# The attention mix in fp32 on half-width columns of the array, with V and the scores kept whole instead of in two parts

## The chip, the cores and the metric

The kernel runs on one core of a Trainium2 chip. The time is the device time of one launch in microseconds: the median of three runs for the kernel before is 313.22 us (313.04 to 313.24).

The core has five engines with a queue each: PE (TensorE, the matmuls; PEld is its weight load), DVE (VectorE), ACT (ScalarE), POOL (GpSimd) and SP (which here issues the loads of the weights). They meet through semaphores.

## The reference

One transformer layer over 256 tokens, 1024 wide, 16 heads of 64, all in fp32. One MoBA block is 256 long, so only a token's own block remains and the attention is plain causal attention with a relative-position bias:

```
y   = rms_norm(x, attn_norm)
qkv = y @ w_qkv                                   # 1024 x 3072
s   = q @ k.T / 8 + rel_bias[bucket(i - j)]       # causal, per head
p   = softmax(s);   o = p @ v
h   = x + o @ w_o
u   = causal_conv3(rms_norm(h, ffn_norm) @ w_up) + conv_b      # 1024 x 5632
h   = h + (silu(gate) * val) @ w_down             # 2816 x 1024
out = rms_norm(h, final_norm)
```

## The kernel before

The large matmuls run in fp32r, a one-pass form of the matmul with a shortened mantissa. To keep nearly all of fp32, each operand is split into two parts: ACT writes a high part (rounded to fp32r), DVE writes the low part (value minus high part), and PE sums three products: high by high, high by low, low by high. The weights come from HBM in 1 MB pieces (`raw`, issued by SP), and each half piece is split by `split_hi` (L141, ACT, tile `whi`) and `split_lo` (L154, DVE, tile `wlo`) some steps ahead of their use. All instructions stand in the order in which the code writes them; there is no scheduler.

The stages: the V projection (256 tokens by 1024, in four PSUM accumulators), then a loop over the eight pairs of heads (p = 0 to 7), then the output projection, then the FFN and the last norm.

In step p of the loop PE runs `project(p, 0)` (Q of the pair, 24 matmuls of 256 columns), `mix(p-3)`, `scores(p-1)`, `project(p, 1)` (K, 24 matmuls) and `flip(p-2)`. After the loop, `mix(5)`, `scores(7)`, `flip(6)`, `mix(6)`, `flip(7)` and `mix(7)` stand among the matmuls of the output projection (`o_part`). So five mixes in the loop and `mix(5)` after it are followed by a `scores`; `mix(6)` is followed by a `flip`, `mix(7)` by `o_part`.

What these do:

- `scores(p)` is four true fp32 matmuls (tiles `qt`, `kt`): for each of the two heads of the pair, one with 128 and one with 256 moving columns. A head has 64 channels, so each matmul uses 64 of the array's 128 rows; head 0 takes the lower half, head 1 the upper. The trace has two PE records for each fp32 matmul (two passes, each with its own weight load), so eight for a pair. DVE adds the bias and takes the row maximum (L401, L405), ACT takes the exponential (L410), and `normalise` divides by the sum on DVE (L414, L418).
- `flip(p)` transposes the pair's scores: six fp32 transposes on PE (L423 to L425) into a two-bank PSUM tile; ACT copies them to the high part of `pt` (L427), DVE makes the low part (L428).
- `mix(p)` multiplies by V. The stationary operand is the pair's 128 columns of V (both heads), in a high and a low part (`vs`, 2 parts x 2 token blocks x 1024); the moving operand is the flipped scores of both heads side by side (512 columns for the first 128 keys, 256 for the last 128, which only later queries see). Three part products of two matmuls make six. Each head's result is then half of the output: rows 0 to 63 of head 0's columns and rows 64 to 127 of head 1's; the other halves are not used. Four evictions, ACT two (L443, high part of `ot`) and DVE two (L445, low part), each on 64 partitions.

`vs` itself is written after the V projection by four ACT (L350) and four DVE (L351) instructions. `pt` has one buffer.

Of the kernel before, what the change touches and what calls it, by code (L numbers as in the profile page):

```python
# [8 lines left out]
F32 = mybir.dt.float32  # L9
F32R = mybir.dt.float32r  # L10
BF16 = mybir.dt.bfloat16
AF = mybir.ActivationFunctionType
ALU = mybir.AluOpType

P = 128
S = 256
NT = S // P
D = 1024
KD = D // P
H = 16  # L20
HD = 64
NP = H // 2
# [16 lines left out]
def bucket_of(d):  # L39
    exact = BUCKETS // 2  # L40
    if d < exact:
        return d
    big = exact + int(math.log(d / exact) / math.log(MAX_DIST / exact) * (BUCKETS - exact))
    return min(big, BUCKETS - 1)
# [3 lines left out]
def tile_block(ctx: ExitStack, tc, x, attn_norm, w_qkv, w_o, rel_bias, ffn_norm, w_up, conv_w,  # L48
               conv_b, w_down, final_norm, out):
    nc = tc.nc  # L50
# [12 lines left out]
    def acc():  # L63
        return psA.tile([P, 512], F32, name="acc")

    def bank():
        return psW.tile([P, 512], F32, name="bank")

    def two_banks():
        return psT.tile([P, 1024], F32, name="twobank")  # L70

    def mm(o, lhsT, rhs, start, stop):
        nc.tensor.matmul(o, lhsT, rhs, start=start, stop=stop, skip_group_check=True)  # L73
# [169 lines left out]
    def rstds():  # L243

        r = small.tile([P, NT], F32, name="rstd")
        nc.vector.scalar_tensor_tensor(r, stat[:, 0, :], D * EPS, stat[:, 1, :], op0=ALU.add, op1=ALU.add)
        nc.gpsimd.tensor_tensor(r, r, minus_half.to_broadcast([P, NT]), op=ALU.pow)
        return r

    def spread(d, ps):  # L250

        for t in range(NT):
            mm(ps[:, t * P:(t + 1) * P], ones, d[t], True, True)
        return ps[:, :S]

    def diagonals(r):
        d = [small.tile([P, P], F32, name=f"diag{t}", bufs=1) for t in range(NT)]
        for t in range(NT):
            nc.vector.tensor_scalar(d[t], ident, r[:, t:t + 1], None, op0=ALU.mult)
        return d  # L260
# [31 lines left out]
    while d1 >= 0:  # L292
        b = bucket_of(d1)
# [3 lines left out]
        n = d1 - d0 + 1  # L297
# [6 lines left out]

    att = ctx.enter_context(ExitStack())
    ap = att.enter_context(tc.tile_pool(name="ap", bufs=1))
    vs = ap.tile([P, 2, NT, D], F32R, name="vs")
    ot = ap.tile([P, 2, NP, S], F32R, name="ot")
    ap.tile([P, 48], F32, name="skew")
    rk, rq = (ap.tile([P, S], F32, name=n) for n in ("rk", "rq"))  # L310
# [19 lines left out]
    accs = {c: acc() for c in CHAINS}  # L330
# [3 lines left out]
    for i in range(4):  # L334
# [8 lines left out]
        if i == 2:  # L343
            nc.scalar.activation(junk[1], xt[1], AF.Square, accum_out=stat[:, 0, 1:2])
            r1 = rstds()
            d1 = diagonals(r1)
    ps = spread(d1, bank())
    for t, half in CHAINS:
        c = slice(half * 512, (half + 1) * 512)
        nc.scalar.activation(vs[:, 0, t, c], accs[t, half], AF.Copy, scale=r1[:, t:t + 1])  # L350
        nc.vector.scalar_tensor_tensor(vs[:, 1, t, c], accs[t, half], r1[:, t:t + 1], vs[:, 0, t, c].bitcast(F32),  # L351
                                       op0=ALU.mult, op1=ALU.subtract)
    nc.vector.tensor_copy(rk, ps)
    nc.vector.tensor_scalar(rq, rk, HD ** -0.5, None, op0=ALU.mult)
    unit(2)
# [6 lines left out]
    def backwards(a):  # L362

        (step, n), _ = a.ap
        return bass.AP(tensor=a.tensor, offset=a.offset + P - 1, ap=[[step, n], [P, NT], [-1, P]])

    qt, kt, sc, pt, bias, sums = {}, {}, {}, {}, {}, {}
# [52 lines left out]
    def flip(p):  # L420
        ps = two_banks()
        for a in range(2):
            nc.tensor.transpose(ps[:, a * S:a * S + P], sc[p][:, a, 0:P], ident)  # L423
            nc.tensor.transpose(ps[:, a * S + P:(a + 1) * S], sc[p][:, a, P:2 * P], ident)  # L424
            nc.tensor.transpose(ps[:, 512 + a * P:512 + (a + 1) * P], sc[p][:, a, 2 * P:], ident)  # L425
        pt[p] = ap.tile([P, 2, 768], F32R, name="pt", bufs=1)
        nc.scalar.activation(pt[p][:, 0, :], ps[:, :768], AF.Copy)  # L427
        nc.vector.tensor_tensor(pt[p][:, 1, :], ps[:, :768], pt[p][:, 0, :].bitcast(F32), op=ALU.subtract)  # L428

    def mix(p):  # L430
        ps = acc() if p < NP - 2 else bank()
        c = slice(p * P, (p + 1) * P)
        late = ps.rearrange("p (a q) -> p a q", a=2)[:, :, P:]
        for n, (i, j) in enumerate(((0, 0), (1, 0), (0, 1))):
            mm(ps, vs[:, i, 0, c], pt[p][:, j, :512], n == 0, False)
            mm(late, vs[:, i, 1, c], pt[p][:, j, 512:].rearrange("p (a q) -> p a q", a=2), False, n == 2)
        for i in range(2):
            for a in range(2):
                r = slice(a * HD, (a + 1) * HD)
                o = backwards(ps[r, a * S:(a + 1) * S])  # L440
                h, l = (ot[r, n, p, :].rearrange("p (t q) -> p t q", t=NT) for n in range(2))
                if i == 0:
                    nc.scalar.activation(h, o, AF.Copy)  # L443
                else:
                    nc.vector.tensor_tensor(l, o, h.bitcast(F32), op=ALU.subtract)  # L445

# [4 lines left out]
    for p in range(NP):  # L453
        split_to(("qk", p))
        project(p, 0)
        if p >= 3:
            mix(p - 3)
        if p >= 1:
            scores(p - 1)
            unit_lo()  # L460
        project(p, 1)
        if p == 0:
            other_params()
        if p >= 2:
            flip(p - 2)
        if p >= 1:
            normalise(p - 1)
            unit_hi()
        unit()
        if p + 2 < NP:  # L470
            load_bias(p + 2)
        split_to(("qk", p), AHEAD)

    accs = {}
# [7 lines left out]

    o_part(0, 0, range(0, 5))
    mix(NP - 3)
    scores(NP - 1)
    unit_lo()
    flip(NP - 2)
    normalise(NP - 1)
    unit_hi()
    o_part(1, 0, range(0, 5))  # L490
    o_part(0, 0, [5])
    o_part(1, 0, [5])
    mix(NP - 2)
    split_to(("up", 0))
    flip(NP - 1)
    o_part(0, 1, range(0, 5))
    o_part(1, 1, range(0, 4))
# [38 lines left out]
    accs = {}  # L536
# [71 lines left out]
    ps = spread(diagonals(rstds()), acc())  # L608
# [3 lines left out]
    for j in range(NF):  # L612
# [7 lines left out]
        i = (j - 3) // 2  # L620
# [87 lines left out]
```

## Time and profile before

| | |
|---|---|
| median of three runs | 313.22 us (313.04 to 313.24) |
| the profiled execution | 312.95 us, of which the span is 311.2 us |
| PE busy | 302.1 us (97%) |
| DVE busy, ACT busy | 241.8 us (78%), 179.7 us (58%) |
| granted clock of PE over the span | 0.996 |

The span is the time from the first to the last instruction of the profiled execution. A matmul's record is longer than what it adds to a row of matmuls, since they are pipelined: what one costs in a row is the distance from its start to the start of the next. The timeline merges neighbouring records that share names; its second column runs from the first record's start to the last one's end.

### The profile page before, as it was taken

Reading aid. Unit: us, or ns where it says so; the run is one execution under the profiler, and the core shown is the slowest. Engines: PE = TensorE matmul, PEld = TensorE weight load, DVE = VectorE, ACT = ScalarE, POOL = GpSimd, SP = SyncE. Lnnn points to the kernel's source line nnn. Section 1 sums busy time; section 2 is a strip of 40 time slices with the busy share of each in tenths; the row PEclk is TensorE's granted clock in tenths of the full one; section 3 lists DMA queues with packets and bytes.
Section 4 is the critical chain, followed back from the end, with each engine's and each line's share of the span. In section 5 each row is a group of like instructions: output and inputs, shape, how many; then the busy total and the mean of one; then the engine's idle time right before and its main releaser. Section 6 shows DMA issues by size and latency. Waiting matters only on the chain.

```text
span 311.2 us, 5486 instructions
## 1 busy us (share of the span) xinstructions
PE 302.1 (97%) x2150; PEld 276.2 (89%) x2150; DVE 241.8 (78%) x460; ACT 179.7 (58%) x322; POOL 17.3 (6%) x55
## 2 busy tenths in 40 slices
PE   7999999999999999999999999999999999999991
PEld 7678999999988788999998989898989999999881
DVE  2476897898888785499989695989595959599762
ACT  4575567555566774557757474757373737365221
POOL 4602000000000000000000000000000000000000
PEclk9999999999999999999999999999999999999998
DMA  7997296808443365247476647567473847500011
GB/s 236 416 371 256 70 332 223 293 22 260 135 132 119 134 191 214 72 145 257 145 267 184 223 142 266 168 238 269 135 273 135 259 149 222 185 2 0 0 70 67
DMA packets 38902, 56.58 MB, mean 182 GB/s; under 512 B 1164, under 2 KB 32604, under 8 KB 38876
## 3 DMA queue, kind: packets, MB, share of 16 engines
q1 hardware_dynamic: 37724, 53.05, 50.4%
q0 software_dynamic: 848, 2.65, 3.0%
q10 hardware_dynamic: 304, 0.53, 0.4%
q8 instruction: 17, 0.28, 0.3%
q14 instruction: 9, 0.07, 0.1%
HBM read 55.15 MB, written 1.07 MB: 181 GB/s over the span
## 4 chain that ended last, share of the span: by engine, by line
PE 90%; DMA 3%; issue 3%; DVE 2%; SPq 1%; ACT 1%; POOLq 0%; POOL 0%; DVEq 0%
PE acc L73 44%; PE bank L73 43%; DMA raw<-in_w_qkv_dram 3%; PE twobank L73 1%; PE twobank L424 1%; PE twobank L423 1%; PE twobank L425 1%; DVE xs L635 0%; PE bank L267 0%; SPq L193 0%; DVE wlo L154 0%; ACT whi L141 0%; DVE yt L272 0%; PE acc L267 0%; ACT yt L269 0%
## 5 line engine op out<-in xcount | busy, mean ns | idle before, releaser
L73 PE MATMUL bank<-yt,whi 128*128 128x256 f32 x720 | 123.4, 277 | 0.1
L154 DVE TENSOR_TENSOR wlo<-raw,whi 128x1024 fp32r<-128x1024 f32 x98 | 117.0, 1219 | 1.7 <-ACT whi L141 1.6
L73 PEld LDWEIGHTS bank<-yt,whi 128*128 128x128 f32 x720 | 108.4, 188 | 0.5 <-ACT yt L269 0.5
L141 ACT ACTIVATE whi<-raw 128x1024 fp32r<-128x1024 f32 x98 | 98.0, 1048 | 4.4 <-DMA raw<-in_w_qkv_dram 4.1
L73 PE MATMUL bank<-yt,wlo 128*128 128x256 f32 x360 | 99.4, 276 | 0.0
L73 PEld LDWEIGHTS bank<-yt,wlo 128*128 128x128 f32 x360 | 67.6, 188 | 0.0
L570 ACT ACTIVATE cv<-u,params 128x256 f32<-128x256 f32 x44 | 24.1, 595 | 65.7 <-DVE u L566 65.7
L73 PE MATMUL acc<-whi,at 128*128 128x512 f32 x164 | 44.8, 390 | 0.0
L73 PE MATMUL acc<-yt,whi 128*128 128x256 f32 x224 | 40.4, 283 | 0.0
L73 PEld LDWEIGHTS acc<-yt,whi 128*128 128x128 f32 x224 | 33.8, 188 | 2.4 <-issue 2.3
L73 PEld LDWEIGHTS acc<-whi,at 128*128 128x128 f32 x164 | 30.1, 188 | 5.8
L566 DVE TENSOR_TENSOR u<-bank,rb 128x512 f32<-128x512 f32 x22 | 15.2, 691 | 21.1 <-PE bank L73 21.1
L73 PE MATMUL acc<-yt,wlo 128*128 128x256 f32 x112 | 31.1, 277 | 0.0
L410 ACT ACTIVATE sc<-sc,nm 128x128 f32<-128x128 f32 (+1 forms) x32 | 14.2, 445 | 22.1 <-DVE nm L405 22.1
L73 PE MATMUL acc<-wlo,at 128*128 128x512 f32 (+1 forms) x90 | 26.1, 370 | 0.0
L582 DVE SCALAR_TENSOR_TENSOR cv<-u,params,cv 128x254 f32<-128x254 f32 x44 | 21.3, 483 | 1.6
L580 DVE SCALAR_TENSOR_TENSOR cv<-u,params,cv 128x255 f32<-128x255 f32 x44 | 21.1, 478 | 0.3 <-ACT cv L570 0.3
L73 PEld LDWEIGHTS acc<-yt,wlo 128*128 128x128 f32 x112 | 21.0, 188 | 0.0
L73 PE MATMUL acc<-whi,ot 128*128 128x512 f32 x64 | 20.1, 396 | 0.0
L73 PEld LDWEIGHTS acc<-wlo,at 128*128 128x128 f32 x90 | 16.9, 188 | 3.5
L73 PE MATMUL acc<-whi,yt 128*128 128x512 f32 x64 | 17.9, 398 | 0.2 <-DVE yt L272 0.2
L428 DVE TENSOR_TENSOR pt<-twobank,pt 128x768 fp32r<-128x768 f32 x8 | 7.7, 958 | 9.5 <-ACT pt L427 9.4
(119 smaller groups left out, 306.6 us busy)
## 6 DMA issues: line engine op xcount, KB each, us to landing
raw<-in_w_up_dram SPq DMA_DIRECT2D x22, 1024.0 KB, 5.3
raw<-in_w_qkv_dram SPq DMA_DIRECT2D x11, 1024.0 KB, 8.4
raw<-in_w_down_dram SPq DMA_DIRECT2D x11, 1024.0 KB, 4.9
raw<-in_w_o_dram SPq DMA_DIRECT2D x4, 1024.0 KB, 7.0
bias<-line_d POOLq DMA_DIRECT2D x8, 256.0 KB, 4.9
raw<-in_w_qkv_dram SPq DMA_DIRECT2D x2, 512.0 KB
xs<-in_x_dram SPq DMA_DIRECT2D x2, 256.0 KB
xs<-in_x_dram SPq DMA_DIRECT2D x1, 512.0 KB
```

What stands on the lines that cost most here:

```text
L73: nc.tensor.matmul(o, lhsT, rhs, start=start, stop=stop, skip_group_check=True)
L141: nc.scalar.activation(h, src, AF.Copy)
L154: nc.vector.tensor_tensor(l, src, h, op=ALU.subtract)
L410: nc.scalar.activation(sc[p][:, a, c], sc[p][:, a, c], AF.Exp, bias=nm[:, j], accum_out=z[:, j])
L423: nc.tensor.transpose(ps[:, a * S:a * S + P], sc[p][:, a, 0:P], ident)
L424: nc.tensor.transpose(ps[:, a * S + P:(a + 1) * S], sc[p][:, a, P:2 * P], ident)
L425: nc.tensor.transpose(ps[:, 512 + a * P:512 + (a + 1) * P], sc[p][:, a, 2 * P:], ident)
L428: nc.vector.tensor_tensor(pt[p][:, 1, :], ps[:, :768], pt[p][:, 0, :].bitcast(F32), op=ALU.subtract)
L566: nc.vector.tensor_tensor(u, ps, rb2.unsqueeze(1).to_broadcast([P, 2, S]), op=ALU.mult)
L570: nc.scalar.activation(c[:, a, :], u[:, a, :], AF.Identity, scale=w2, bias=b)
L580: nc.vector.scalar_tensor_tensor(c[:, a, 1:], u[:, a, :S - 1], w1, c[:, a, 1:], op0=ALU.mult, op1=ALU.add)
L582: nc.vector.scalar_tensor_tensor(c[:, a, 2:], u[:, a, :S - 2], w0, c[:, a, 2:], op0=ALU.mult, op1=ALU.add)
```

## The change

V is written once, in fp32: its left half of columns by ACT, its right half by DVE (two instructions each). The flipped scores are copied once by ACT, into one of two `pt` buffers, and have no low part. `mix` runs four fp32 matmuls: for each block of keys and each head, the head's 64 columns of V are the stationary operand and only that head's scores move. Head 0's output goes to PSUM partitions 0 to 63, which takes the lower 64 columns of the array, head 1's to partitions 64 to 127, the upper 64 columns; all 128 rows of the array are used. One ACT and one DVE instruction on 128 partitions then write the two parts of `ot`. All else is the same.

```
-    vs = ap.tile([P, 2, NT, D], F32R, name="vs")
+    vs = ap.tile([P, NT, D], F32, name="vs")
...
-        nc.scalar.activation(vs[:, 0, t, c], accs[t, half], AF.Copy, scale=r1[:, t:t + 1])
-        nc.vector.scalar_tensor_tensor(vs[:, 1, t, c], accs[t, half], r1[:, t:t + 1], vs[:, 0, t, c].bitcast(F32),
-                                       op0=ALU.mult, op1=ALU.subtract)
+        if half == 0:
+            nc.scalar.activation(vs[:, t, c], accs[t, half], AF.Copy, scale=r1[:, t:t + 1])
+        else:
+            nc.vector.tensor_scalar(vs[:, t, c], accs[t, half], r1[:, t:t + 1], None, op0=ALU.mult)
...
-        pt[p] = ap.tile([P, 2, 768], F32R, name="pt", bufs=1)
-        nc.scalar.activation(pt[p][:, 0, :], ps[:, :768], AF.Copy)
-        nc.vector.tensor_tensor(pt[p][:, 1, :], ps[:, :768], pt[p][:, 0, :].bitcast(F32), op=ALU.subtract)
+        pt[p] = ap.tile([P, 768], F32, name="pt", bufs=2)
+        nc.scalar.activation(pt[p], ps[:, :768], AF.Copy)
 
     def mix(p):
-        ps = acc() if p < NP - 2 else bank()
-        c = slice(p * P, (p + 1) * P)
-        late = ps.rearrange("p (a q) -> p a q", a=2)[:, :, P:]
-        for n, (i, j) in enumerate(((0, 0), (1, 0), (0, 1))):
-            mm(ps, vs[:, i, 0, c], pt[p][:, j, :512], n == 0, False)
-            mm(late, vs[:, i, 1, c], pt[p][:, j, 512:].rearrange("p (a q) -> p a q", a=2), False, n == 2)
-        for i in range(2):
+        ps = (acc() if p < NP - 2 else bank())[:, :S]
+        for i, q in ((0, slice(0, S)), (1, slice(P, S))):
             for a in range(2):
                 r = slice(a * HD, (a + 1) * HD)
-                o = backwards(ps[r, a * S:(a + 1) * S])
-                h, l = (ot[r, n, p, :].rearrange("p (t q) -> p t q", t=NT) for n in range(2))
-                if i == 0:
-                    nc.scalar.activation(h, o, AF.Copy)
-                else:
-                    nc.vector.tensor_tensor(l, o, h.bitcast(F32), op=ALU.subtract)
+                v = vs[:, i, p * P + a * HD:p * P + (a + 1) * HD]
+                b = pt[p][:, a * S:(a + 1) * S] if i == 0 else pt[p][:, 512 + a * P:512 + (a + 1) * P]
+                mm(ps[r, q], v, b, i == 0, i == 1)
+        h, l = (ot[:, n, p, :].rearrange("p (t q) -> p t q", t=NT) for n in range(2))
+        nc.scalar.activation(h, backwards(ps), AF.Copy)
+        nc.vector.tensor_tensor(l, backwards(ps), h.bitcast(F32), op=ALU.subtract)
```

How the instructions stand on PE at the first mix of the loop (p = 3), before: the end of Q's projection (`yt` by `whi`, `wlo`), the mix (`acc` from `pt` and `vs`), the scores of the next pair (`bank` from `kt` and `qt`), the start of K's projection.

```order
L73 MATMUL acc_686<-yt_121,wlo_484 128x256
L73 MATMUL acc_713<-pt_667,vs_174 128x512
L73 MATMUL acc_713<-pt_667,vs_174 128x2x128
...
L73 MATMUL bank_726<-kt_658,qt_608 128x128
L73 MATMUL bank_727<-kt_658,qt_608 128x128
L73 MATMUL bank_726<-kt_658,qt_608 128x256
L73 MATMUL bank_727<-kt_658,qt_608 128x256
L73 MATMUL acc_745<-yt_121,whi_482 128x256 x2
```

(The two rows of the mix stand three times in turn; they are shown once.) The same place in the changed kernel:

```order
L73 MATMUL acc_681<-yt_121,wlo_480 128x256
L73 MATMUL acc_708<-pt_663,vs_174 64x256 x2
L73 MATMUL acc_708<-pt_663,vs_174 64x128 x2
L73 MATMUL bank_717<-kt_654,qt_604 128x128
L73 MATMUL bank_718<-kt_654,qt_604 128x128
L73 MATMUL bank_717<-kt_654,qt_604 128x256
L73 MATMUL bank_718<-kt_654,qt_604 128x256
L73 MATMUL acc_736<-yt_121,whi_478 128x256 x2
```

The mix is in the same place, in four fp32 matmuls of 64 output partitions each instead of six of 128; nothing around it moves. On DVE, in the last step with scores (p = 7, after the loop), before: the bias and maximum of the scores are followed by a weight split, the low part of the flipped scores of pair 6 and then the division of pair 7's scores, for which the next flip waits.

```order
L405 TENSOR_SCALAR nm_1281<-mx_1270 128x4
L154 TENSOR_TENSOR wlo_1288<-raw_906,whi_1236 128x1024
L428 TENSOR_TENSOR pt_1297<-twobank_1290,pt_1297 128x768
L414 RECIPROCAL rz_1300<-z_1283 128x4
L418 TENSOR_SCALAR sc_1269<-sc_1269,rz_1300 128x128
...
L445 TENSOR_TENSOR ot_175<-bank_1330,ot_175 64x256 x2
```

The same place in the changed kernel:

```order
L406 TENSOR_SCALAR nm_1247<-mx_1236 128x4
L154 TENSOR_TENSOR wlo_1254<-raw_891,whi_1206 128x1024
L415 RECIPROCAL rz_1265<-z_1249 128x4
L419 TENSOR_SCALAR sc_1235<-sc_1235,rz_1265 128x128
...
L441 TENSOR_TENSOR ot_175<-bank_1295,ot_175 128x256
```

The low part of `pt` is gone from between the split and the division (the division's other three instructions, in both, are left out here), and the low part of `ot` is one instruction instead of two.

## Rows read from the trace of the kernel before

**Rows 1.** The page: span, and busy time of each engine (share of the span, instructions).
```profile
span 311.2 us, 5486 instructions
PE 302.1 (97%) x2150; PEld 276.2 (89%) x2150; DVE 241.8 (78%) x460; ACT 179.7 (58%) x322; POOL 17.3 (6%) x55
```

**Rows 2.** The page: chain that ended last, share of the span by engine.
```profile
PE 90%; DMA 3%; issue 3%; DVE 2%; SPq 1%; ACT 1%; POOLq 0%; POOL 0%; DVEq 0%
```

**Rows 3.** Waits of the weight loads: who waited for whom, total us, times, longest us.
```profile
PEld bank L73 <- DVE pt L428: 0.3, 1, 0.3
PEld acc L73 <- DVE pt L428: 0.3, 1, 0.3
```

**Rows 4.** Timeline of PE around a mix: start, us, engine, line, op, out<-in, shape, count.
```profile
63.21 0.39 PE L73 MATMUL acc<-yt,whi 128*128 128x256 f32 x2
63.44 0.28 PE L73 MATMUL acc<-yt,wlo 128*128 128x256 f32 x1
63.55 1.21 PE L73 MATMUL acc<-pt,vs 128*128 128x512 f32 x6
64.69 0.93 PE L73 MATMUL bank<-kt,qt 64*128 64x128 f32 x8
65.55 0.51 PE L73 MATMUL acc<-yt,whi 128*128 128x256 f32 x2
65.89 0.28 PE L73 MATMUL acc<-yt,wlo 128*128 128x256 f32 x1
```

**Rows 5.** The same scores in three narrow windows, to part the eight records.
```profile
64.69 0.38 PE L73 MATMUL bank<-kt,qt 64*128 64x128 f32 x2
...
65.02 0.60 PE L73 MATMUL bank<-kt,qt 64*128 64x256 f32 x4
...
65.23 0.38 PE L73 MATMUL bank<-kt,qt 64*128 64x256 f32 x2
```

**Rows 6.** Timeline of PE where scores follow a projection without a mix.
```profile
41.48 0.28 PE L73 MATMUL acc<-yt,wlo 128*128 128x256 f32 x1
41.69 0.93 PE L73 MATMUL bank<-kt,qt 64*128 64x128 f32 x8
```

**Rows 7.** Timeline of PE: fp32 passes of 128 columns on the whole array.
```profile
4.99 1.73 PE L73 MATMUL twobank<-ident,ones 128*128 128x128 f32 x14
6.55 0.62 PE L267 MATMUL bank<-ident,xs 128*128 128x128 f32 x4
```

**Rows 8.** Timeline of PE at the last mix.
```profile
113.47 1.22 PE L73 MATMUL bank<-pt,vs 128*128 128x512 f32 x6
114.52 0.62 PE L73 MATMUL acc<-whi,ot 128*128 128x512 f32 x2
```

**Rows 9.** Timeline of PE at the fifth mix of the loop.
```profile
88.33 1.44 PE L73 MATMUL acc<-pt,vs 128*128 128x512 f32 x6
89.70 0.93 PE L73 MATMUL bank<-kt,qt 64*128 64x128 f32 x8
```

**Rows 10.** Timeline of all engines at the mix of pair 6 and the flip after it.
```profile
104.02 0.81 ACT L427 ACTIVATE pt<-twobank 128x768 fp32r<-128x768 f32 x1
...
104.87 0.96 DVE L428 TENSOR_TENSOR pt<-twobank,pt 128x768 fp32r<-128x768 f32 x1 [1.65 <-ACT pt L427]
105.02 1.47 PE L73 MATMUL bank<-pt,vs 128*128 128x512 f32 x6
105.74 0.17 DVE L414 RECIPROCAL rz<-z 128x4 f32<-128x4 f32 x1
105.94 1.01 DVE L418 TENSOR_SCALAR sc<-sc,rz 128x128 f32<-128x128 f32 x4
106.38 0.30 PE L423 MATMUL twobank<-ident,sc 128*128 128x128 f32 x1
...
107.20 0.72 PE L73 MATMUL acc<-whi,ot 128*128 128x512 f32 x2
```

**Rows 11.** Timeline of PE at a flip in the loop: its first record and what follows it.
```profile
60.16 0.27 PE L423 MATMUL twobank<-ident,sc 128*128 128x128 f32 x1
...
60.73 0.48 PE L73 MATMUL acc<-yt,whi 128*128 128x256 f32 x2
```

## The prediction

> **What bounds the kernel now.** I read the busy times first: PE is at 97% of the span, DVE at 78%, ACT at 58% [rows 1]. The chain of waits says the same: 90% of it is PE [rows 2]. So work taken from DVE or ACT is worth only the waits of PE that it ends, and the list of PE's waits has just two that name what the change removes, the low part of the flipped scores (L428): 0.3 us each [rows 3]. What counts is the length of the mix on PE. For that I went through the timeline of PE at a mix, at scores with and without a mix ahead, and at the three places where a mix or a flip is longer than its sisters. The trace agrees with itself: three matmuls of 256 columns go from 63.21 to 63.55, 0.11 us each, without a gap [rows 4], and PE holds that pace through the loop.
>
> **The mix on PE, before.** In the loop the six matmuls take from 63.55 to 64.69, 1.14 us to the first record of the scores [rows 4]. A part of that is the step into half-array work: a projection's last matmul is followed by the scores after 0.21 us [rows 6] where 0.11 is its own, so 0.10 us is lost at such a switch. Where a mix runs into whole-array work it takes 113.47 to 114.52, 1.05 us [rows 8].
>
> **The mix on PE, after.** Four fp32 matmuls of two passes each, four records of 256 and four of 128 columns, two halves of the array. The trace has no column halves; the nearest row is the scores: also four fp32 matmuls, four records of 128 and four of 256 columns, two halves, there of rows. They take from 64.69 to 65.55, 0.86 us to the next work [rows 4]. Inside it the halves run beside each other: two records begin at 64.69, four of 256 columns fill 65.02 to 65.62 with the second two beginning at 65.23, so 256 columns of both halves pass in 0.21 us and 128 in about half of that [rows 5]. The eight records stream 2 x 0.21 + 2 x 0.11 = 0.64 us; the other 0.22 is the first weight load (64.69 to 65.02 is 0.33 for two passes of 128 columns, 0.11 more than they need) and the 0.10 to 0.11 of leaving. The lower end of the price is this with less load, because a half has 64 columns of weights to load and not 128: 0.05 less if the load goes with the columns. The upper end is no overlap at all. A whole-array fp32 pass of 128 columns costs 1.56 us / 14 = 0.11 [rows 7], so the eight records one after the other stream 4 x 0.21 + 4 x 0.11 = 1.28 us instead of 0.64, 1.50 in all. I take 0.86, since the row it comes from is the same work but for the direction of the halves.
>
> On this the TensorE page of the Trainium skill ("TensorE: Matmul & The Clock Gate", Part 3, under measured speedup) has three column tiles at 2.38 times one, which goes with the lower end; no row here shows column tiles. The same part, under what overlaps, says that matmuls start strictly in program order. The trace does not bear that out for row halves. The code gives a head's matmul and then the other head's, and each is two passes; in strict order the first head's second pass would stand ahead of the other head's first, and the two records that begin at 64.69 [rows 5] would not begin together. What that rule would make of column halves is a rival below.
>
> To the 0.86 comes the step into half-array work ahead of the mix, 0.10 [rows 6]; the one behind it is inside the 0.86, as it was inside the 1.14.
>
> - Six mixes with scores behind them: 0.10 + 0.86 = 0.96 against 1.14, -0.18 each, -1.08 us.
> - Two mixes with whole-array work behind them: there the next weight load is not ahead any more. After the scores two matmuls take 65.55 to 65.89, 0.34 [rows 4], where 0.23 is the pace, so 0.11 is added: 0.10 + 0.86 + 0.11 = 1.07 against 1.05 [rows 8], +0.02 each, +0.04 us.
>
> A lost 0.10 at the switch from column to row halves, were it larger than what whole to row costs, would add up to 0.10 x 6; were there none, it would take off as much. I take it as the same.
>
> **Waits that go.** The third part product needs the low part of `pt`, and that goes. The fifth mix takes 88.33 to 89.70, 1.37 [rows 9], 0.23 above 1.14. The mix of pair 6 takes 105.02 to 106.38, 1.36, 0.31 above 1.05: L428 began only at 104.87 and took 0.96 [rows 10]. The flip right after is slow too, 106.38 to 107.20, 0.82 [rows 10], against 0.57 for one in the loop [rows 11]; its transposes run behind the four divisions, which stood behind L428 on DVE and began at 105.94 [rows 10]. Without L428 the divisions are 0.96 earlier and the flip keeps its pace: -0.25. Together -0.23 - 0.31 - 0.25 = -0.79 us. What is late next is ACT's copy of `pt`, done at 104.83, against the mix at 105.02 [rows 10]: 0.19 us of room. The mix comes some 0.9 us earlier (five mixes at 0.18), but the copy hangs on the scores before it, which move along, and on DVE ahead of them, which loses L428 and one of two low parts of `ot`. If that failed, 0.1 to 0.3 us would come back.
>
> **Edits with no price.** V whole, split between ACT and DVE: fewer instructions on both, and PE waits for neither in any row. Two `pt` buffers of half the size: the copy waits for less. One eviction of 128 partitions instead of two of 64: same columns, half the instructions. All of this lies beside PE at 97%. No DMA is added or moved; freed engines split weights a little earlier, which issues loads earlier, and after the start PE waits for none. What of this would cost anything if the cover went is nothing, since each only shortens.
>
> **Sum.** -1.08 + 0.04 - 0.79 = -1.83 us. Against the profiled execution (span 311.2, time 312.95): 311.1. The median of the runs shown is 0.27 above that execution: 311.4. Shorter weight loads, 0.05 x 8, could take off 0.4. I forecast 311.3 us. Its own range: with short loads and no lost time from column to row halves 310.3; with the waits only half gone and 0.10 more lost at each of the eight mixes 312.6.
>
> **Rivals.**
>
> *The halves run, but only in part beside each other.* If a second pass could not be overtaken, the 256-column passes would need three slots instead of two (first; second beside the other head's first; the other's second): +0.21 a mix, 8 x 0.21 = +1.7, so 313.0, no change. That is what the strict order quoted above would give. The same page says that weight loads overlap running matmuls only where the row group differs, and column halves share all rows. As a mechanism here: three more loads of a mix lie open, at 0.05 to 0.11 each, 8 x 3 of them, +1.2 to +2.6, so 312.5 to 313.9. For it: no row shows column halves. Against it: in the scores the two halves start together and only the first load lies open [rows 5].
>
> *The halves take turns (the other side).* If work on column halves that share their rows cannot run together, each mix streams 1.28 instead of 0.64 us: 8 x 0.64 = +5.1, so 316.4, slower than before. It decides as soon as more than a third of the overlap is missing, 1.83 / 5.1. For it: each half streams its own moving operand over all 128 rows, where the scores' halves share none, and fp32 is the heaviest stream there is. Against it: the array works in halves of rows at full pace [rows 5].
>
> *The change does not do what it says for PE:* a new wait in place of L428, for ACT's copy of `pt`, at all mixes. 0.19 us of room at pair 6 [rows 10] was the least that I found; 0.3 us at some mixes would be +1 us, 312.3.
>
> **Chances.** Halves beside each other, 0.60; in part, 0.18; taking turns, 0.17; a new wait, 0.05. A change of 0.2%, 0.63 us, is about what a measurement here can tell from none: faster is below 312.6, slower above 313.85. The first case is faster but for 0.03; the second is faster with 0.03, same with 0.13, slower with 0.02; the third is slower; the last faster with 0.02, same with 0.03. Faster 0.62, same 0.19, slower 0.19. The range, 310.2 to 313.9, holds the first two cases and the last, and leaves out the turns.
>
> **What would show it.** In the profile after, the records of the mix: if the halves overlap, pairs of records with 64 columns begin within a few ns, and from the first record of a mix to the first of the scores it is 0.8 to 0.9 us; in part, 1.0 to 1.15; in turns, 1.4 to 1.5. The step from the last projection matmul into the mix should be 0.21. The waits for L428 are gone with it; the flip after mix 6 is 0.57 long. PE's busy share stays near 97%, and nothing behind the attention changes its length. The forecast is wrong if a mix with its step in costs over 1.14 us, or if the mixes shorten and a wait for `pt`, `whi` or `wlo` appears on PE.

## The result and the profile after

The changed kernel takes 310.44 us in the median (309.95 to 311.39, 6 runs), the kernel before 313.19 beside it (312.46 to 313.56): a ratio of 0.9917 [0.9904, 0.9930], 2.75 us less. Run twice more beside the kernel before, it came to 310.85 and 310.79 us, 0.9941 [0.9923, 0.9959] and 0.9933 [0.9914, 0.9952], so what it saves is 1.9 to 2.75 us. The forecast was 311.3 us in a range of 310.2 to 313.9. The profiled execution took 310.05 us. Since single runs scatter by some 0.7 us, I read causes from steps in the traces, and times only as their confirmation.

The page of the profile after: the span, and the busy time of each engine [rows 1].

```profile
span 308.3 us, 5486 instructions
PE 299.5 (97%) x2166; PEld 273.5 (89%) x2166; DVE 231.7 (75%) x442; ACT 175.6 (57%) x312; POOL 17.2 (6%) x55
```

PE is as full as before; its work got shorter, by 2.6 us. The chain that ended last still has 90% of PE in it [rows 2].

Two waits of the weight loads after that are new from the loop on (who waited for whom, total us, times, longest us):

```profile
PEld bank L73 <- DVE qt L386: 0.7, 4, 0.2
...
PEld bank L73 <- ACT whi L141: 0.4, 1, 0.4
```

The waits for the low part of `pt` [rows 3] are gone, and none for `pt` from ACT stands in their place. The four for `qt`, 0.17 us each, are no loss on PE: they are the pause of the weight loads at a change from mix to scores. At the first mix of the loop the same 0.17 us stands there without a wait for `qt` (it is put down to "issue"), and all five mixes of the loop take 0.80 us. The one for `whi`, one of the prediction's signs of being wrong, is no loss either: it is the pause at the last mix, 0.35 us, and the two mixes before it have the same 0.35 put down to "issue".

The timeline of PE after, around the mix in the loop that answers to [rows 4]:

```profile
62.76 0.28 PE L73 MATMUL acc<-yt,wlo 128*128 128x256 f32 x1
62.96 0.87 PE L73 MATMUL acc<-pt,vs 128*64 128x256 f32 x8
63.76 0.93 PE L73 MATMUL bank<-kt,qt 64*128 64x128 f32 x8
```

From the projection's last matmul to the mix it is 0.20 us, from the mix's first record to the scores 0.80. The same eight records in two narrow windows:

```profile
62.96 0.44 PE L73 MATMUL acc<-pt,vs 128*64 128x256 f32 x2
...
63.23 0.60 PE L73 MATMUL acc<-pt,vs 128*64 128x256 f32 x6
```

Two records begin together at 62.96, and the next ones at 63.23: the pairs come 0.27 us apart where a pass of 256 columns takes 0.21, so 0.05 to 0.06 of a weight load lies open once. In the scores it was about 0.11 [rows 5]; there a half has 128 columns of weights, here 64, and the record of one weight load in this trace is 0.136 us here and 0.187 there. After that the eight records stream with nothing between them.

The copy of `pt` for pair 6 on ACT and its mix (timeline of all engines, other rows left out), against [rows 10]:

```profile
100.70 0.79 ACT L428 ACTIVATE pt<-twobank 128x768 f32<-128x768 f32 x1
...
102.94 0.87 PE L73 MATMUL bank<-pt,vs 128*64 128x256 f32 x8
```

The copy ends at 101.49, 1.45 us ahead of its mix, where it had 0.19.

Where the time went is read best in the chain that ended last, whose pieces are the same in both kernels (start us, us, what, how many instructions). Before; x30 is a projection with the mix behind it, x21 a part of the output projection with a mix:

```profile
60.98 3.79 PE acc L73 x30
64.76 0.86 PE bank L73 x8
65.62 2.96 PE acc L73 x24
...
85.75 4.01 PE acc L73 x30
...
94.22 4.50 PE acc L73 x21
...
105.18 0.69 PE bank L73 x4
...
107.44 6.18 PE acc L73 x27
113.63 1.06 PE bank L73 x6
114.68 6.16 PE acc L73 x27
```

After:

```profile
60.29 3.54 PE acc L73 x32
63.83 0.86 PE bank L73 x8
64.69 2.95 PE acc L73 x24
...
84.29 3.54 PE acc L73 x32
...
92.29 4.25 PE acc L73 x23
...
103.00 0.80 PE bank L73 x8
...
104.61 6.15 PE acc L73 x27
110.77 0.80 PE bank L73 x8
111.57 6.39 PE acc L73 x27
```

- Four of the five mixes of the loop: 3.79 to 3.54, -0.25 each, -1.00.
- The fifth: 4.01 to 3.54, -0.47; 0.22 of it is the wait [rows 9].
- The mix of pair 5: 4.50 to 4.25, -0.25.
- The mix of pair 6 with its flip: 105.18 to 107.44 is 2.26, 103.00 to 104.61 is 1.61: -0.65.
- The last mix with the work behind it: 1.06 + 6.16 = 7.22 and 0.80 + 6.39 = 7.19, -0.03.

Together -2.40 us. At the two mixes behind the loop the chain has 0.80 where [rows 8] had 1.05, but the work behind takes some of it back: 6.39 for 6.16, and 0.26 for the flip's first transpose. The two spans differ by 2.9; 0.28 of the rest is the first load of weights, which took 9.02 us in the one execution and 8.74 in the other, ahead of anything that the change touches. The last 0.2 I have not traced.

### The profile page after: what moved, and what is told of

The parts are those of the page before. It is cut to its first block, busy times and chain, and to the rows that moved or that the text cites. A ratio compares the mean times of both kernels' runs of the same rounds, so it can differ in the third digit from the quotient of the medians.

```text
span 308.3 us, 5486 instructions
## 1 busy us (share of the span) xinstructions
PE 299.5 (97%) x2166; PEld 273.5 (89%) x2166; DVE 231.7 (75%) x442; ACT 175.6 (57%) x312; POOL 17.2 (6%) x55
## 4 chain that ended last, share of the span: by engine, by line
PE 90%; DMA 3%; issue 3%; DVE 2%; SPq 1%; ACT 1%; POOLq 0%; POOL 0%; DVEq 0%
PE acc L73 43%; PE bank L73 43%; DMA raw<-in_w_qkv_dram 3%; PE twobank L73 1%; PE twobank L424 1%; PE twobank L425 1%; PE twobank L426 1%; DVE xs L631 0%; PE bank L267 0%; SPq L193 0%; DVE wlo L154 0%; ACT whi L141 0%; DVE yt L272 0%; PE acc L267 0%; ACT yt L269 0%
## 5 line engine op out<-in xcount | busy, mean ns | idle before, releaser
L73 PEld LDWEIGHTS acc<-whi,yt 128*128 128x128 f32 x64 | 11.7, 188 | 2.7 <-DVE yt L272 0.4
```

## The experiments

Three questions stood open: is it the column halves that shorten PE's work, or fp32 as such; are the waits worth what I counted; and is the relief of DVE and ACT really worth nothing else? Each run is timed against the kernel before on the same chip (312.83, 312.54 and 312.72 us in the three groups, of which the second, with before_no_low, heads_in_turn, sub_only and evict_four, has no run of the changed kernel, so ratios are compared); diffs are against the changed kernel unless said.

**after_again, after_third.** The changed kernel as it is, to compare with.

> The changed kernel itself, on the chip of the three runs beside it. Theory (the column halves run beside each other, the load of a half is shorter, and the waits for the low part are gone): 310.4 us, 0.992 of the kernel before. From the first record of a mix to the first of the scores 0.80 us.

> The changed kernel once more, on the chip of the three orders of PE's work beside it: 310.4 to 310.9 us, 8.00 us a step of the loop.

Measured: 310.85 (310.32 to 311.47) and 310.79 us (309.96 to 311.70).

**one_half.** Only head 0 of each pair is mixed, in the lower 64 columns of the array; head 1's attention output is left out (zeros).

```diff
-            for a in range(2):
+            for a in range(1):
...
-        h, l = (ot[:, n, p, :].rearrange("p (t q) -> p t q", t=NT) for n in range(2))
...
+        r = slice(0, HD)
+        h, l = (ot[r, n, p, :].rearrange("p (t q) -> p t q", t=NT) for n in range(2))
```

> Half of the mix's work is left out: only head 0 of each pair, on the lower column half; head 1's part of the attention's output is zero. Theory that the two halves run beside each other: PE gains nothing, 0.80 us from a mix's first record to the scores', the time within 0.5 us of the changed kernel (310.4). Rival that the halves take turns for a part of the way: the mix gets shorter by what they did not share; if they shared nothing, by half of the streaming, 0.32 us a mix and 2.6 us in all (307.8).

Measured: 310.22 us (309.86 to 310.69), 0.9920 [0.9902, 0.9938]. PE's timeline at its mix:

```profile
62.50 0.43 PE L73 MATMUL acc<-pt,vs 128*64 128x256 f32 x1
...
62.50 0.86 PE L73 MATMUL acc<-pt,vs 128*64 128x256 f32 x4
63.30 0.93 PE L73 MATMUL bank<-kt,qt 64*128 64x128 f32 x8
```

One record at a time now, half as many, and still 0.80 to the scores. The second head costs PE nothing: the halves run wholly beside each other. Halves that take turns are excluded: they would have made this run 2.6 us shorter. Its median lies 0.63 below that of after_again, but not by the mixes, which differ by 0.01 each in the two chains (3.53 and 3.54).

**heads_in_turn.** Both key blocks of head 0, then both of head 1.

```diff
-        for i, q in ((0, slice(0, S)), (1, slice(P, S))):
-            for a in range(2):
+        for a in range(2):
+            for i, q in ((0, slice(0, S)), (1, slice(P, S))):
```

> The changed kernel with the mix's matmuls in another order: both key blocks of head 0, then both of head 1, so that head 1's first pass stands behind four passes of head 0 and not behind two. Theory (each half of the columns runs at its own pace, far ahead of the other if need be): no change, 0.80 us a mix, 310.4 to 310.9. Rival (a pass overtakes only what stands just ahead): head 1 begins beside head 0's later passes, a mix takes 0.2 to 0.55 us more, +1.7 to +4.3 us.

Measured: 310.02 us (309.79 to 310.31), 0.9915 [0.9899, 0.9930]. Its timeline, the first window narrow:

```profile
62.90 0.44 PE L73 MATMUL acc<-pt,vs 128*64 128x256 f32 x2
...
63.70 0.71 PE L73 MATMUL bank<-kt,qt 64*128 64x128 f32 x6
```

Two records begin together at 62.90, although all four passes of head 0 stand ahead of head 1's first in the program, and a head alone has its records one after the other (one_half). A record does not tell its head, but by that the second of the two is head 1's: its first pass starts ahead of three passes of head 0 that were issued earlier, and the block is 0.80 again. The Trainium skill ("TensorE: Matmul & The Clock Gate", Part 3, under what overlaps) has matmuls strictly in program order and weight loads beside matmuls only for other row groups; for two column halves the trace agrees with neither: the records begin in pairs, and of the loads only the first lies open, by some 0.05 us, although both halves share all rows.

**whole_width.** The mix in fp32 over the whole width of the array, without halves, V and `pt` whole as in the changed kernel; four evictions of 64 partitions come back with it.

```diff
-                mm(ps[r, q], v, b, i == 0, i == 1)
+        mm(ps, vs[:, 0, c], pt[p][:, :512], True, False)
+        mm(late, vs[:, 1, c], pt[p][:, 512:].rearrange("p (a q) -> p a q", a=2), False, True)
```

> The mix in fp32, but on the whole array: both heads' 128 columns of V stationary, both heads' scores moving (512 and 256 columns), so that half of the output is not used, and four evictions on 64 partitions as before. V and pt stay whole, no low part. Theory (the gain on PE is the halves): four records stream 1.28 us; in the loop the mix takes 1.28 to 1.40 to the first record of the scores, 0.4 to 0.5 more than with halves (0.10 of entry and 0.80), at the two last mixes 0.2 to 0.3 more: +2.8 to 3.6 us against the changed kernel, 313.2 to 314.0, no faster than the kernel before. Rival (the gain is the waits that went and the work taken from DVE and ACT): about 310.5 to 311.5.

Measured: 314.50 us (313.49 to 315.37), 1.0052 [1.0032, 1.0071], slower than before the change. Its chain, in the loop and at the last two mixes:

```profile
60.69 4.03 PE acc L73 x28
...
105.80 1.29 PE bank L73 x4
...
107.75 6.16 PE acc L73 x27
113.90 1.29 PE bank L73 x4
115.19 6.17 PE acc L73 x27
```

Against 3.54 that is +0.49 at each of the six mixes with scores behind them. At pair 6 the mix with its flip takes 1.95 against 1.61, +0.34, and the last mix with the work behind it 7.46 against 7.19, +0.27. Together that is +3.55; measured +3.65 against the changed kernel beside it, just above the 2.8 to 3.6 expected. It is the halves that save time on PE; fp32 over the whole width costs more than the three products in two parts did (3.79).

**before_no_low.** The kernel before, without the low part of `pt`; its third product takes the high part again (so PE has the same work; the small term of that product is left out, and the large product counts twice in the result).

```diff
-        nc.vector.tensor_tensor(pt[p][:, 1, :], ps[:, :768], pt[p][:, 0, :].bitcast(F32), op=ALU.subtract)
...
-        for n, (i, j) in enumerate(((0, 0), (1, 0), (0, 1))):
+        for n, (i, j) in enumerate(((0, 0), (1, 0), (0, 0))):
```

> The kernel before, without DVE's low part of the flipped scores: the third product of each mix takes the high part again, so the low part's share is missing from the result. PE does the same work. Theory (this part of the gain is waits on the chain from DVE to ACT and back): the waits of the fifth mix, of the mix of pair 6 and of the flip behind it go, 0.8 us, and the loop's chain falls to PE's pace: 312.0 to 312.5 where the kernel before has 312.8 to 313.2. Rival (the waits only look like waits; their time returns elsewhere): no change.

Measured: 311.88 us (311.49 to 312.54), 0.9977 [0.9966, 0.9988], -0.66, a little better than the 312.0 to 312.5 expected. Its chain at the fifth mix and at pair 6:

```profile
85.46 3.79 PE acc L73 x30
...
104.68 1.06 PE bank L73 x6
...
106.40 6.13 PE acc L73 x27
```

The fifth mix is like its sisters (3.79, not 4.01), and pair 6 with its flip takes 1.72 instead of 2.26: -0.22 - 0.54 = -0.76.

**side_work.** The changed kernel with the old work on DVE and ACT: a subtraction of 768 columns into a buffer that nobody reads, and four evictions of 64 partitions.

```diff
+        nc.vector.tensor_tensor(spare, ps[:, :768], pt[p], op=ALU.subtract)
...
-        nc.scalar.activation(h, backwards(ps), AF.Copy)
-        nc.vector.tensor_tensor(l, backwards(ps), h.bitcast(F32), op=ALU.subtract)
+        for n in range(2):
+            for a in range(2):
+                ...
```

> The changed kernel with DVE's and ACT's work around pt and ot put back: DVE also subtracts for each pair (768 columns, into a spare tile that nothing reads), and the four evictions on 64 partitions stand in place of two on 128. PE waits for none of the subtraction. Theory (only waits of PE count): the mixes stay at 0.80 us; the divisions of the last pair come a subtraction later again, so the flip after the mix of pair 6 loses up to 0.25 us: 310.4 to 310.8. Rival (freeing DVE and ACT is itself worth most of the gain): 312 or more.

Measured: 313.60 us (312.66 to 314.49), 1.0024 [1.0010, 1.0038]. This expectation, and with it a step of my prediction, fell: with the old side work the whole gain is gone, 2.75 us against after_again. The subtraction in its timeline of DVE:

```profile
63.09 0.96 DVE L430 TENSOR_TENSOR spare<-twobank,pt 128x768 f32<-128x768 f32 x1 [1.37 <-ACT pt L429]
...
80.22 0.96 DVE L430 TENSOR_TENSOR spare<-twobank,pt 128x768 f32<-128x768 f32 x1 [1.37 <-ACT pt L429]
```

The second is two steps behind the first: it comes every 17.13 / 2 = 8.57 us, where a step of PE in the changed kernel is 8.00 (3.54 + 0.86 + 2.95 in its chain above, and six transposes of 0.11). Its chain that ended last no longer runs through PE here:

```profile
77.80 1.57 ACT sc L412 x7
79.38 0.82 ACT pt L429
80.22 0.96 DVE spare L430
...
83.78 0.33 DVE ot L449
```

Exponentials and the copy of `pt` on ACT; the subtraction, the divisions, a split of weights, `qt` and the low part of `ot` on DVE; then the scores' additions and the next exponentials: a ring through the two engines, each waiting in turn for the other. With 78% and 58% busy over the span [rows 1], and 83% and 61% in these steps of the kernel before, neither looks like a bound. Looking back, the same ring stands in the kernel before, in the starts of L428 on DVE:

```profile
62.61 0.96 DVE L428 TENSOR_TENSOR pt<-twobank,pt 128x768 fp32r<-128x768 f32 x1 [1.37 <-ACT pt L427]
...
88.14 0.96 DVE L428 TENSOR_TENSOR pt<-twobank,pt 128x768 fp32r<-128x768 f32 x1 [1.31 <-ACT pt L427]
```

Three steps lie between these two: (88.14 - 62.61) / 3 = 8.51 us a step, against PE's 8.26 (3.79 + 0.86 + 2.96 and six transposes of 0.11). The ring lost 0.25 us of its lead in each step until the fifth mix had to wait. In before_no_low, without the subtraction, the copy of `pt` comes every 8.26 us (69.50, 77.76, 86.03): PE's pace. The two waits that I had listed were the end of that.

**sub_only, evict_four.** The two halves of side_work, each alone: only the line with `spare`, or only the four evictions.

> The changed kernel with DVE's subtraction of 768 columns a pair put back alone (into a spare tile that nothing reads). The run with all the side work cost 2.75 us, and in its trace the subtraction comes every 8.56 us, a chain from DVE to ACT and back, where PE alone needs 8.00 for a step of the loop. Theory (that chain is what costs): without the two extra evictions it is 8.56 - 0.43 = 8.13 a step, still 0.13 over PE's 8.00, and the flip after the mix of pair 6 waits: +0.4 to +1.5 us against the changed kernel, 311.2 to 312.3. Rival (the cost is in the evictions on 64 partitions): no more than 0.3 us.

> The changed kernel with only the four evictions on 64 partitions put back in place of two on 128. Theory (chain from DVE to ACT and back): about 7.2 + 0.43 = 7.6 us a step against PE's 8.00, so it stays hidden: the changed kernel's time within 0.4 us (310.4 to 310.9). Rival (the evictions are what costs in the run with all the side work): 1.5 us or more.

Measured: 310.65 (310.15 to 310.91) and 310.98 us (310.82 to 311.08), 0.9933 [0.9918, 0.9948] and 0.9943 [0.9928, 0.9957]: the changed kernel's time. The subtraction in sub_only:

```profile
61.33 0.96 DVE L430 TENSOR_TENSOR spare<-twobank,pt 128x768 f32<-128x768 f32 x1 [1.23 <-ACT pt L429]
...
77.10 0.96 DVE L430 TENSOR_TENSOR spare<-twobank,pt 128x768 f32<-128x768 f32 x1 [1.23 <-ACT pt L429]
```

Two steps again, 15.77 / 2: its ring turns in 7.88 us, less than 8.00, so it costs nothing; I had expected 0.4 to 1.5. By difference the two more evictions add 8.57 - 7.88 = 0.69 to it, where I had taken 0.43. In evict_four PE's steps are 8.00 too. Neither alone is felt, both together cost 2.75 us: the ring is either under PE's step or over it.

**flip_first, flip_after_scores, mix_apart.** Where else could the mix or the flip stand on PE? Flip ahead of the mix; flip right behind the scores; mix between K's projection and the flip, away from the scores.

```diff
         if p >= 3:
+            flip(p - 2)
             mix(p - 3)
...
-        if p >= 2:
-            flip(p - 2)
+        if p == 2:
+            flip(0)
```

```diff
             scores(p - 1)
+        if p >= 2:
+            flip(p - 2)
+        if p >= 1:
             unit_lo()
...
-        if p >= 2:
-            flip(p - 2)
```

```diff
-        if p >= 3:
-            mix(p - 3)
         if p >= 1:
             scores(p - 1)
...
         project(p, 1)
+        if p >= 3:
+            mix(p - 3)
```

> The changed kernel with the flip of a step moved ahead of its mix (from p = 3 on, and for pair 6 after the loop), so that a step has flip, mix and scores in a row: the switch from transposes back to a projection (0.09 us) goes, none is added. Theory (each switch of PE between kinds of work costs its 0.1 us whatever else runs): 7.91 us a step, -0.5 us in all against the changed kernel. Rival (the flip comes ahead of the division it needs, and PE waits): no gain, or slower.

> The changed kernel with the flip moved to right after the scores instead of after K's projection. Theory: the way out of the scores falls together with the transposes' first load, 0.05 us a step less, 7.95, -0.3 us in all. Rival (a flip so early holds the two-bank PSUM tile or ACT): slower.

> The changed kernel with the mix of the loop moved from ahead of the scores to behind K's projection, ahead of the flip. Theory (a switch costs 0.1 us, and so it matters that mix and scores are neighbours): one more entry and an exposed load of the transposes, 0.15 us a step, 8.15, +0.75 us in all. Rival (going into column halves costs nothing of its own): 8.00 a step, no change.

Measured: 310.69 us (310.61 to 310.98), 0.9931 [0.9915, 0.9947]; 311.50 (310.97 to 311.96), 0.9952 [0.9934, 0.9970]; 312.20 (311.86 to 312.75), 0.9977 [0.9966, 0.9989]. The chain of flip_after_scores and then that of mix_apart:

```profile
65.01 0.26 PE twobank L424
```

```profile
60.06 2.83 PE acc L73 x24
...
63.74 3.83 PE acc L73 x32
67.57 0.26 PE twobank L424
```

A flip's first transpose is 0.26 behind scores or a mix, 0.11 behind a projection; that makes steps of 8.12 instead of 8.00. Apart from the scores the mix costs more: 2.83 for a projection that was 3.54 - 0.80 = 2.74, 3.83 where 2.95 + 0.80 = 3.75 would be, and 0.15 at the flip: +0.32 together, and its steps are 8.31 to 8.32. The flip ahead of the mix saves 0.03 a step (steps of 7.97), not the 0.09 that I expected; its time can't be told from the changed kernel's. "TensorEngine Tiling (Array Packing)" in the Trainium skill, key properties, says that a change of tiling mode drains the engine, and gives no price; here a loss of 0.1 to 0.15 us at each change agrees with that, and neighbours of the half-array kind are worth 1.4 us of the whole. None of these beats the changed kernel, nor does heads_in_turn by more than the scatter.

## Why the prediction was right

The forecast of 311.3 lies 0.9 us above the first median and 0.5 above the two later ones.

- *Six mixes with scores behind them.* Predicted 0.10 + 0.86 = 0.96 against 1.14, -0.18; measured -0.25 each, -1.50 and not -1.08. The mechanism holds: pairs begin together, one load lies open. The mis-sized term is the 0.86 taken from the scores: the block is 0.80. The lower end that the prediction named, 0.05 less because a half has 64 columns of weights, was the right one, and the load's record is shorter by as much (0.136 against 0.187).
- *The two mixes with whole-array work behind them.* Predicted +0.04; -0.03 for the last one, and for pair 6, compared without its waits (1.72 in before_no_low, 1.61 after), -0.11. The same 0.06 a mix; at pair 6, besides, the load that lies open behind the mix, taken at 0.11, was about 0.06. The flip there is 0.63 long (103.74 to 104.37 in the timeline) and not the 0.57 named among the signs: its first transpose comes 0.06 later behind a mix in halves.
- *Waits that go.* Predicted -0.79; before_no_low has -0.76 in its trace and -0.66 in the median. Right in size, and the rival of a new wait for `pt` fell: the copy has 1.45 us of room at pair 6.
- *Halves in part, in turns.* Excluded by one_half and heads_in_turn: 0.80 with one half or two, and in either order of issue.
- *"Edits with no price."* This step failed: "All of this lies beside PE at 97%", and with it the sentence that work taken from DVE or ACT is worth only the waits of PE that it ends. What the edits take from DVE and ACT is the condition of the gain. The halves alone, with the old side work (side_work), give 313.60 against 312.83, no gain (up to 0.7 of that may be the pace of the last section, which leaves none either); the low part alone gives -0.66; both together -1.98 in the same group as side_work. My sum came out since the change relieves the ring by more than it needed, subtraction and evictions both, so that PE's shorter step could count in full. That the change brought this relief with it was luck as far as the prediction goes, which never read the ring's pace. Had the change left that work in place, the same reasoning would have forecast about 312 and missed.

Sum: -1.83 predicted, -2.40 in the trace's pieces; 8 x 0.06 = 0.48 of the difference is the one term.

## What to carry to other kernels

Two fp32 matmuls of 64 output columns that share their rows can be issued to two column halves, and then cost the time of one, 0.80 us for the block with one head or two; put them beside other half-array work, since each change of kind cost 0.1 to 0.15 us here. Before shortening PE's step, read how often one instruction of each helper engine comes round: a ring through two engines at 78% and 58% turned in 8.51 us where PE needed 8.26, and with its old work it took all of the gain (side_work). The waits that showed only at the last steps of the loop were a lead that had been used up in all of them, and the work that used it up cost more once PE's step was shorter: 2.75 us (side_work) against 0.66 (before_no_low).

## What the runs showed of the hardware

Between executions PE's pace differs in one stretch with the granted clock at 1.00, its upper level. The chain of the changed kernel at 124 to 145 us, in the first profile and then in after_third:

```profile
124.18 5.46 PE bank L73 x48
...
130.08 13.61 PE bank L73 x120
```

```profile
124.39 5.66 PE bank L73 x48
...
130.49 14.13 PE bank L73 x120
```

The same matmuls take 0.113 us each in the one and 0.118 in the other, 0.72 us together, most of the 0.9 between the two spans. The slower pace is in nine of the eleven profiles of kernels with column halves, and in none of the three without (the kernel before, before_no_low, whole_width), so of the distance of side_work to the kernel before up to 0.7 may be this and not the ring; its steps, at 8.57, do not hang on it. One profile of a kernel is too few to say whether the halves bring it about (that of whole_width is the fastest of its seven runs, 313.49 against a median of 314.50, so its other runs may differ), and no run was made for it: the cause stays open.
